# Latent depthwise convolution on 32x64 array tiles, and the scan's decay rows loaded from ScalarE's queue

## The chip, the cores and the metric

The kernel runs on one core of one Trainium2 chip. A core has a matrix engine (TensorE, "PE" in the profile; its loads of the stationary operand are "PEld"), VectorE ("DVE"), ScalarE ("ACT"), GpSimd ("POOL") and a queue processor (SyncE, "SP") that here issues all DMAs. Each engine works through its own list of instructions in order, and semaphores tie the lists together. The metric is the device time of the whole kernel in microseconds (us), as the median of several runs; less is better.

## The reference, cut to what matters

One layer of a diffusion backbone is applied to 256 context tokens and to 2048 latent tokens, which form a grid of 32 rows by 64 columns. An input projection feeds two branches: a bidirectional state-space scan (SSD) and a Conformer branch; an output projection joins them. The change touches two places, the depthwise convolution of the Conformer branch on the latent grid, and a load in the scan.

```
def depthwise_conv(x, w, b):            # w: 31 taps x 1024 channels
    k, ch = w.shape
    out = lax.conv_general_dilated(x, w.reshape(k, 1, 1, ch), window_strides=(1, 1),
        padding=((k // 2, k // 2), (0, 0)), dimension_numbers=('NHWC', 'HWIO', 'NHWC'),
        feature_group_count=ch)
    return out + b

def conformer_branch(ga, gb, conv_w, conv_b, ln_g, ln_b):   # latent: (1, 32, 64, 1024)
    h = ga * jax.nn.sigmoid(gb)
    h = depthwise_conv(h, conv_w, conv_b)
    h = layer_norm(h, ln_g, ln_b)
    return jax.nn.silu(h)
```

The taps run along the grid's rows only. So for one channel the convolution is a product of the 64 x 32 grid (columns by rows) with a banded 32 x 32 matrix that is made of that channel's taps. In the scan, per head and chunk of 128 tokens, `decay_in = exp(segsum(la))` is a 128 x 128 matrix, made from one row of running sums (the decay row) that is laid over all partitions.

## The kernel before, in words

Tokens come in 18 tiles of 128 (two of context, sixteen latent). The work has two halves: tiles 0 to 9, then 10 to 17. In each half a phase of the input projection (`xbc_phase`) feeds the scan, and a second one (`post`: `gab_unit` for the gates, `silu_unit` for the rest) runs while the scan of that half (`scan`, `pass_a`) is woven in between its matmuls. The projection's matmuls are L378 to L380, three for each 128-row slice, with 512 moving columns. They give TensorE a dense stream, and everything else is put between them by hand: `interleave` and `merge` advance the generators of the scan and of the convolutions one step at a time after so many projection steps. The framework then orders each engine's list by a simulated timeline on the basis of that order (`schedule_with_timeline_sim=True`). After the second half come the output projection and the norms (L1078 and what is around it), to the end.

The latent convolution runs in the second half only, 8 groups of 128 channels (`lat_conv`, L603 to L645), one after another, with the context convolution (`ctx_conv`, VectorE) between them; the list of these steps (`extra`) is merged with 63 scan steps over 344 projection steps. A group does this:

- L607 loads the bias rows; L611 loads `kd`, for each channel its 32 x 32 band matrix, read with overlapping rows from the padded taps; L616 loads `cx`, the gated grid, from `GL` in DRAM, where `gab_unit` (L540) stored it. Partition `c4*32 + r` holds grid row `r` of every fourth channel, so the four 32-partition quarters hold four channels. `kd` and `cx` have one buffer each (`bufs=1`).
- `expand` (L622): ScalarE copies the small matrices onto the diagonal of a zeroed 128 x 128 operand (`kbuf`, two buffers, cleared once by GpSimd), so that one matmul serves four channels at once. Four copies make the operand for 8 matmul calls, 16 copies a group.
- L634: 32 calls a group; the stationary operand is the grid (128 x 64), the moving one the block-diagonal matrix (128 x 128), the result 64 grid columns by 4 channels x 32 rows. The halves `h` go to the lower and the upper 64 result partitions. A call in plain float32 appears in the profile as two instructions.
- L639: VectorE evicts each result bank, halves it, adds the bias and writes it in the order row, channel (`cvv`); L644 stores that to `CVL` in DRAM.

The scan's step (`pass_a`): `load_lb` (L664) loads the decay rows of 4 heads, broadcast to 128 partitions, into `lb`, one tile for each direction, each with 4 buffers, 8 loads a token tile. `mask` (ScalarE L673, GpSimd L676), `decay` (ScalarE L684, 4 exponentials) and `mix` (VectorE L688, L689) turn them into decay matrices, and `diag` (TensorE L720) uses them. A buffer is free again after L688 (one direction) or L720 (the other). Result banks are split in 3 ("mm", for the projection) and 5 ("ss", for everything else: `px`, `py`, `po`, `pst`, `pb` of the scan, `cps`, and the convolution's `cp`).

```
    extra = chain(f for j in range(4) for f in (lat_conv(2 * j, lp, kbuf), ctx_conv(j + 4, cg), lat_conv(2 * j + 1, lp, kbuf)))
    interleave(take(blocks, 344), merge(sc_, 63, extra, 8 * 6 + 4 * 13), 344)
```

Of the kernel before, what the change touches and what calls it, by code (L numbers as in the profile page):

```python
# [17 lines left out]
P = 128  # L18
# [49 lines left out]
def backbone_kernel(ctx, tc, xa, xt_in, cols, rows, wconv, conf_b, gp_row, bg_row, state0, w_mod, w_dt, w_in, w_out,  # L68
# [458 lines left out]

    def gab_unit(half, j, hb):
        wb = next_w()
        wa = next_w()  # L530
        for b in ORDER[half]:
            BN, o = BNS[b], TOK[b]
            pg = bank("mm", f"gb{half}_{j}_{b}")
            yield from mm_cm(pg, wb, hb[b])
            th = ev(f"gth{half}_{j}_{b}")[:, :BN]
            S.activation(th, pg[:, :BN], AF.Tanh, scale=0.5)  # L536
            pa_ = bank("mm", f"ga{half}_{j}_{b}")
            yield from mm_cm(pa_, wa, hb[b])
            V.scalar_tensor_tensor(th, th, 1.0, pa_[:, :BN], ADD, MUL)  # L539
            DMA.dma_start(GL[j][:, o:o + BN], th)  # L540

# [61 lines left out]
    def lat_conv(j, lp, kbuf):  # L603
        cbb = lp.tile([P, HD], F32, tag="cbb", name=f"cbb{j}", bufs=2)
        for h in range(2):
            c0 = j * P + h * 64
            DMA.dma_start(cbb[h * 64:(h + 1) * 64], conf_b[c0:c0 + 64].partition_broadcast(64))  # L607
        kd = lp.tile([P, 32, 32], F32, tag="kd", name=f"kd{j}", bufs=1)
        for c4 in range(4):
            src = bass.AP(tensor=wconv.tensor, offset=(j * 4 + c4) * 64 * 32, ap=[[32, 32], [1, 1024]])  # L610
            DMA.dma_start(kd[c4 * 32:(c4 + 1) * 32].rearrange("p r g -> p (r g)"), src)  # L611

        x = lp.tile([P, 32, 64], F32, tag="cx", name=f"cx{j}", bufs=1)
        src = GL[j][:, 256:].rearrange("(g c) (r w) -> c r g w", c=4, w=64)
        for c4 in range(4):
            DMA.dma_start(x[c4 * 32:(c4 + 1) * 32], src[c4])  # L616

        def expand(u):
            kt = kbuf[u % 2]
            for c4 in range(4):  # L620
                rs = slice(c4 * 32, (c4 + 1) * 32)
                S.copy(kt[rs, :, rs].rearrange("p (h q) r -> p h q r", h=2),  # L622
                       kd[rs].rearrange("p r (h u q) -> p u h q r", h=2, u=4)[:, u])

        vt = lp.tile([P, 32, HD], F32, tag="cvv", name=f"cvv{j}", bufs=1)
        yield
        expand(0)
        yield
        for u in range(4):
            kt = kbuf[u % 2]  # L630
            ps = bank("ss", f"cp{j}_{u}")
            for q in range(4):
                for h in range(2):
                    T.matmul(ps[h * 64:(h + 1) * 64, q * P:(q + 1) * P], x[:, h * 16 + u * 4 + q, :], kt[:, h * 4 + q, :],  # L634
                             start=True, stop=True)
            if u < 3:
                expand(u + 1)
            yield
            V.scalar_tensor_tensor(vt[:, ::-1, u * 16:(u + 1) * 16].rearrange("p r c -> p c r"),  # L639
                                   ps.rearrange("p (c r) -> p c r", r=32), 0.5,  # L640
                                   cbb[:, u * 16:(u + 1) * 16].unsqueeze(2).to_broadcast([P, 16, 32]), MUL, ADD)
# [3 lines left out]
        yield  # L645


    def pass_a(i):
# [11 lines left out]
        def load_lb(g, hq):  # L660
            for d in range(2):
                lb = pa.tile([P, 4, P], F32, tag=f"lb{d}", name=f"lb{i}{g}{hq}{d}", bufs=4)
                r0 = il * 32 + d * NH + g * 8 + hq * 4
                DMA.dma_start(lb.rearrange("p h l -> p (h l)"),  # L664
# [197 lines left out]
    def chain(gens):  # L862
        for g in gens:
            yield from g
# [64 lines left out]
    kbuf = [lp.tile([P, 8, P], F32, name=f"kbuf{u}") for u in range(2)]  # L929
    for u in range(2):  # L930
        G.memset(kbuf[u], 0.0)
    blocks = post(1, 5)
    cg = lambda name: lp.tile([P, D], F32, tag="cg", name=name, bufs=2)
    extra = chain(f for j in range(4) for f in (lat_conv(2 * j, lp, kbuf), ctx_conv(j + 4, cg), lat_conv(2 * j + 1, lp, kbuf)))
# [295 lines left out]
```

## Time and profile before

| what | value |
|---|---|
| median of 3 runs | 1877.12 us (1874.78 to 1882.59) |
| the profiled execution: time | 1882.2 us |
| its span, first to last instruction | 1880.5 us |
| its mean granted TensorE clock | 0.986 |
| matmuls of the latent convolution (L634) | 512, from 957.8 to 1336.9 us |
| ScalarE's copies for them (L622) | 128, 83.3 us busy |
| loads of decay rows (L664) | 144, on SP's queue |
| first scan beside the projection | about 275 to 700 us |
| second scan, with the latent convolution | about 935 to 1340 us |

How to read the profile. Rows of groups have the line, engine and operation, the tiles as out<-in, the shape (partitions x elements) and the count; behind the first bar the busy time in us and the mean duration of one in ns, behind the second the engine's idle time just before them and what ended it. For matmuls the shape begins with rows*columns of the stationary operand. Rows of a stretch give for each engine its busy time and, in brackets, its instructions, then the granted TensorE clock, the busy share of the DMA engines and GB/s. Rows in order of time begin with start and duration in us; a count at the end means that so many of a kind were put together, from the first start to the last end. Rows of one tile give the shortest, the median and the longest duration in ns. Rows of waits give who waited for whom: us in total, how often, the longest. "SPq" is SP's list, where the duration is what it took to issue a DMA.

### The profile page before, as it was taken

To read this page: it belongs to the slowest core of one execution; us is meant where nothing else is said; L and a number is where in the kernel's file an instruction comes from. 1 tells how busy PE (TensorE), PEld (TensorE's weight loads), DVE (VectorE), ACT (ScalarE), POOL (GpSimd) and SP (SyncE) were. 2 spreads that over 40 slices of the span, in tenths; PEclk is the share of its full clock that TensorE was granted. 3 is DMA by queue.
4 is the path that set the end of the run, shared out by engine and by line. 5 is a ranking of instruction groups with operands and counts; after the bars stand their busy time and mean duration, and the time that the engine had idled before them with its cause. 6 is when DMAs were issued, how large, how long until landed. Compare 5 with 4: busy or idle time off the path is not lost.

```text
span 1880.5 us, 26833 instructions
## 1 busy us (share of the span) xinstructions
PE 1825.6 (97%) x9739; PEld 1504.6 (80%) x9739; DVE 1188.2 (63%) x1699; ACT 839.5 (45%) x1786; POOL 269.0 (14%) x351
## 2 busy tenths in 40 slices
PE   7899999999999999999999899999999999999998
PEld 4788887787887888888877677777887888888887
DVE  2477887776545553577585768655427676766662
ACT  3646424443455441644355666675414232232321
POOL 0002001111111100100001011110013333333220
PEclk9899999999999999999999999999999999999999
DMA  8556575564677754545587897978887655555532
GB/s 302 212 200 198 211 239 179 176 222 155 211 269 225 225 200 169 165 154 188 179 195 215 210 242 194 278 185 234 239 268 239 191 174 173 165 172 173 175 102 78
DMA packets 290400, 375.29 MB, mean 200 GB/s; under 512 B 85206, under 2 KB 187478, under 8 KB 290268
## 3 DMA queue, kind: packets, MB, share of 16 engines
q1 hardware_dynamic: 290268, 373.58, 64.2%
q8 instruction: 77, 1.26, 0.3%
q14 instruction: 55, 0.45, 0.1%
HBM read 243.92 MB, written 129.59 MB: 199 GB/s over the span
## 4 chain that ended last, share of the span: by engine, by line
PE 62%; DMA 5%; ACT 3%; issue 3%; DVE 2%; SPq 2%; POOL 0%; POOLq 0%; DVEq 0%; ACTq 0%
PE op L1078 20%; PE sp L378 6%; PE sp L379 6%; PE sp L380 6%; DMA lb<-lt 3%; PE xp L379 2%; PE xp L378 2%; PE xp L380 2%; PE py L720 2%; PE ga L378 2%; PE ga L380 1%; PE po L727 1%; PE ga L379 1%; PE qo L985 1%; PE gb L378 1%
## 5 line engine op out<-in xcount | busy, mean ns | idle before, releaser
L684 ACT ACTIVATE lb<-lb,WB 128x128 f32<-128x128 f32 x576 | 184.1, 391 | 150.9 <-POOL lb L676 149.0
L378 PE MATMUL sp<-hh,wh 128*128 128x512 f32 (+1 forms) x640 | 239.7, 375 | 2.6 <-DVE sth L550 2.6
L379 PE MATMUL sp<-hl,wh 128*128 128x512 f32 (+1 forms) x640 | 237.0, 370 | 0.0
L380 PE MATMUL sp<-hh,wl 128*128 128x512 f32 (+1 forms) x640 | 236.7, 370 | 0.2 <-DMA wl<-wld 0.2
L676 POOL TENSOR_SCALAR_AFFINE_SELECT lb<-lb 128x512 f32<-128x512 f32 x144 | 108.7, 760 | 749.7 <-ACT el L673 416.1
L378 PE MATMUL xp<-hh,wh 128*128 128x512 f32 (+1 forms) x480 | 179.1, 375 | 6.1 <-ACT wh L353 4.0
L379 PE MATMUL xp<-hl,wh 128*128 128x512 f32 (+1 forms) x480 | 179.1, 373 | 0.2 <-DVE hl L299 0.2
L380 PE MATMUL xp<-hh,wl 128*128 128x512 f32 (+1 forms) x480 | 179.2, 374 | 0.0
L475 DVE SCALAR_TENSOR_TENSOR cva<-raw,cwh,cva 128x1280 f32<-128x1280 f32 (+1 forms) x96 | 142.7, 1495 | 15.5 <-ACT cva L469 13.6
L378 PEld LDWEIGHTS sp<-hh,wh 128*128 128x128 f32 x640 | 121.0, 189 | 24.3 <-DVE sth L550 3.1
L380 PEld LDWEIGHTS sp<-hh,wl 128*128 128x128 f32 x640 | 121.0, 189 | 21.6 <-DMA wl<-wld 0.7
L379 PEld LDWEIGHTS sp<-hl,wh 128*128 128x128 f32 x640 | 121.2, 189 | 20.1 <-issue 0.5
L378 PE MATMUL gb<-hh,wh 128*128 128x512 f32 (+1 forms) x320 | 121.9, 381 | 3.4 <-DVE gth L539 3.4
L378 PE MATMUL ga<-hh,wh 128*128 128x512 f32 (+1 forms) x320 | 120.4, 376 | 2.6 <-ACT gth L536 2.6
L379 PE MATMUL gb<-hl,wh 128*128 128x512 f32 (+1 forms) x320 | 119.3, 373 | 0.0
L380 PE MATMUL gb<-hh,wl 128*128 128x512 f32 (+1 forms) x320 | 119.1, 372 | 0.0
L380 PE MATMUL ga<-hh,wl 128*128 128x512 f32 (+1 forms) x320 | 118.1, 369 | 0.0
L379 PE MATMUL ga<-hl,wh 128*128 128x512 f32 (+1 forms) x320 | 117.9, 369 | 0.0
L590 DVE SCALAR_TENSOR_TENSOR cg<-cg,cv 128x256 f32<-128x256 f32 x240 | 113.3, 497 | 2.5
L550 DVE SCALAR_TENSOR_TENSOR sth<-sth,sp 128x512 f32<-128x512 f32 (+1 forms) x80 | 50.4, 630 | 98.4 <-ACT sth L549 98.4
L378 PEld LDWEIGHTS xp<-hh,wh 128*128 128x128 f32 x480 | 92.0, 192 | 23.0 <-ACT wh L353 4.8
L688 DVE TENSOR_TENSOR lb<-lb,lb 128x512 f32<-128x512 f32 x72 | 51.6, 717 | 85.6 <-ACT lb L684 55.8
(219 smaller groups left out, 3860.8 us busy)
## 6 DMA issues: line engine op xcount, KB each, us to landing
lb<-lt SPq DMA_DIRECT2D x144, 256.0 KB, 4.2
wr<-in_w_in SPq DMA_DIRECT2D x88, 256.0 KB, 4.9
whd<-wh SPq DMA_DIRECT2D x44, 512.0 KB, 3.4
wld<-wl SPq DMA_DIRECT2D x44, 512.0 KB, 4.7
wh<-whd SPq DMA_DIRECT2D x44, 512.0 KB, 5.2
wl<-wld SPq DMA_DIRECT2D x44, 512.0 KB, 5.6
xT<-xb SPq DMA_DIRECT2D x18, 512.0 KB, 5.4
yp<-yg SPq DMA_DIRECT2D x36, 256.0 KB, 4.5
```

The source lines that it names most:

```text
L378: T.matmul(ps[:, :BN], wh[:, k, :], hh[:, k, :], start=(k == 0), stop=False)
L379: T.matmul(ps[:, :BN], wh[:, k, :], hl[:, k, :], start=False, stop=False)
L380: T.matmul(ps[:, :BN], wl[:, k, :], hh[:, k, :], start=False, stop=(k == KT - 1))
L475: V.scalar_tensor_tensor(a[:, :n], raw[:, t:t + n], cwh[:, ct * 5 + t:ct * 5 + t + 1], a[:, :n], MUL, ADD)
L550: V.scalar_tensor_tensor(th, th, 1.0, ps[:, :BN], ADD, MUL)
L590: V.scalar_tensor_tensor(acc, g[:, t:t + 256], cv[:, w0 + t:w0 + t + 1], acc, MUL, ADD)
L676: G.affine_select(E[g, hq, d], E[g, hq, d], pattern=[[0, 4], [sg, P]], compare_op=ALU.is_ge, fill=NEG, base=0, channel_multiplier=-sg)
L684: S.activation(lb[:, h, :], lb[:, h, :], AF.Exp, bias=WB[:, i, c + h:c + h + 1])
L688: V.tensor_tensor(a, a, E[g, hq, 1], ADD)
L720: T.matmul(py[g][j * HD:(j + 1) * HD, q * P:(q + 1) * P], xt[g][:, h * HD:(h + 1) * HD], E[g, hq, 0][:, t, :], start=True, stop=True)
L727: T.matmul(po[g][:, q * P:(q + 1) * P], Sf[g][:, q * P:(q + 1) * P], bc[:, 2 + g, :], start=True, stop=True)
L1078: T.matmul(pso[n], lhs[:, k % 8, :], w[:, n * 512:(n + 1) * 512], start=(k == 0 and m == 0), stop=(k == 15 and m == 2))
```

## The change

The convolution no longer expands its matrices. Each of the four 32-partition quarters (one channel each) is now a matmul of its own, 32 contraction rows by 64 result partitions, with 32 moving columns: 128 calls a group in place of 32. Quarters `a` and `a + 1` go to two "ss" banks that are taken together; the order is by channel `q`, half `h`, quarter `a`. One ScalarE copy a group (`kt`) turns the band matrices into channel-major, row-reversed order; before, the reversal was made by VectorE's write in L639. The loads are a function of their own (`lat_load`), `kd` and `cx` have two buffers, and group `j + 1` is loaded during group `j` if its gates have been written (`gl_done`). A group has 6 steps in place of 7, so that `extra` has 96 steps in place of 104. In the scan, `load_lb` issues its DMAs on ScalarE's queue.

```diff
--- before.py
+++ after.py
@@ -525,9 +525,12 @@
         for _ in dtp:
             pass
 
+    gl_done = set()
+
     def gab_unit(half, j, hb):
         wb = next_w()
         wa = next_w()
+        gl_done.discard(j)
         for b in ORDER[half]:
             BN, o = BNS[b], TOK[b]
             pg = bank("mm", f"gb{half}_{j}_{b}")
@@ -538,6 +541,8 @@
             yield from mm_cm(pa_, wa, hb[b])
             V.scalar_tensor_tensor(th, th, 1.0, pa_[:, :BN], ADD, MUL)
             DMA.dma_start(GL[j][:, o:o + BN], th)
+        if half:
+            gl_done.add(j)
 
     def silu_unit(half, c0, dst, j, hb, order=None):
         w = next_w()
@@ -600,49 +605,53 @@
         yield
 
 
-    def lat_conv(j, lp, kbuf):
+
+
+    lat_in = {}
+
+    def lat_load(j, lp):
+        kd = lp.tile([P, 32, 32], F32, tag="kd", name=f"kd{j}", bufs=2)
+        x = lp.tile([P, 32, 64], F32, tag="cx", name=f"cx{j}", bufs=2)
         cbb = lp.tile([P, HD], F32, tag="cbb", name=f"cbb{j}", bufs=2)
+        lat_in[j] = kd, x, cbb
         for h in range(2):
             c0 = j * P + h * 64
             DMA.dma_start(cbb[h * 64:(h + 1) * 64], conf_b[c0:c0 + 64].partition_broadcast(64))
-        kd = lp.tile([P, 32, 32], F32, tag="kd", name=f"kd{j}", bufs=1)
-        for c4 in range(4):
-            src = bass.AP(tensor=wconv.tensor, offset=(j * 4 + c4) * 64 * 32, ap=[[32, 32], [1, 1024]])
-            DMA.dma_start(kd[c4 * 32:(c4 + 1) * 32].rearrange("p r g -> p (r g)"), src)
-
-        x = lp.tile([P, 32, 64], F32, tag="cx", name=f"cx{j}", bufs=1)
-        src = GL[j][:, 256:].rearrange("(g c) (r w) -> c r g w", c=4, w=64)
-        for c4 in range(4):
-            DMA.dma_start(x[c4 * 32:(c4 + 1) * 32], src[c4])
-
-        def expand(u):
-            kt = kbuf[u % 2]
-            for c4 in range(4):
-                rs = slice(c4 * 32, (c4 + 1) * 32)
-                S.copy(kt[rs, :, rs].rearrange("p (h q) r -> p h q r", h=2),
-                       kd[rs].rearrange("p r (h u q) -> p u h q r", h=2, u=4)[:, u])
-
+        src = GL[j][:, 256:].rearrange("(g a) (r w) -> a r g w", a=4, w=64)
+        for a in range(4):
+            rs = slice(a * 32, (a + 1) * 32)
+            DMA.dma_start(kd[rs].rearrange("p r g -> p (r g)"),
+                          bass.AP(tensor=wconv.tensor, offset=(j * 4 + a) * 64 * 32, ap=[[32, 32], [1, 1024]]))
+            DMA.dma_start(x[rs], src[a])
+
+    def lat_conv(j, lp, more):
+        if j not in lat_in:
+            lat_load(j, lp)
+        kd, x, cbb = lat_in.pop(j)
+        yield
+        kt = lp.tile([P, 32, 32], F32, tag="kt", name=f"kt{j}", bufs=1)
+        S.copy(kt[:, :, ::-1].rearrange("p g r -> p r g"), kd)
+        if more(j + 1):
+            lat_load(j + 1, lp)
+        yield
         vt = lp.tile([P, 32, HD], F32, tag="cvv", name=f"cvv{j}", bufs=1)
-        yield
-        expand(0)
-        yield
-        for u in range(4):
-            kt = kbuf[u % 2]
-            ps = bank("ss", f"cp{j}_{u}")
-            for q in range(4):
+        for a2 in (0, 2):
+            ps = {a: bank("ss", f"cp{j}_{a}") for a in (a2, a2 + 1)}
+            for q in range(16):
                 for h in range(2):
-                    T.matmul(ps[h * 64:(h + 1) * 64, q * P:(q + 1) * P], x[:, h * 16 + u * 4 + q, :], kt[:, h * 4 + q, :],
-                             start=True, stop=True)
-            if u < 3:
-                expand(u + 1)
+                    for a in ps:
+                        rs = slice(a * 32, (a + 1) * 32)
+                        T.matmul(ps[a][h * 64:(h + 1) * 64, q * 32:(q + 1) * 32], x[rs, h * 16 + q, :], kt[rs, h * 16 + q, :],
+                                 start=True, stop=True)
             yield
-            V.scalar_tensor_tensor(vt[:, ::-1, u * 16:(u + 1) * 16].rearrange("p r c -> p c r"),
-                                   ps.rearrange("p (c r) -> p c r", r=32), 0.5,
-                                   cbb[:, u * 16:(u + 1) * 16].unsqueeze(2).to_broadcast([P, 16, 32]), MUL, ADD)
+            for a in ps:
+                V.scalar_tensor_tensor(vt[:, :, a::4].rearrange("p r c -> p c r"),
+                                       ps[a].rearrange("p (c r) -> p c r", r=32), 0.5,
+                                       cbb[:, a::4].unsqueeze(2).to_broadcast([P, 16, 32]), MUL, ADD)
+            yield
         for h in range(2):
             c0 = j * P + h * 64
             DMA.dma_start(CVL[:, c0:c0 + 64].rearrange("(r w) c -> w r c", w=64), vt[h * 64:(h + 1) * 64])
-        yield
 
 
     def pass_a(i):
@@ -661,7 +670,7 @@
             for d in range(2):
                 lb = pa.tile([P, 4, P], F32, tag=f"lb{d}", name=f"lb{i}{g}{hq}{d}", bufs=4)
                 r0 = il * 32 + d * NH + g * 8 + hq * 4
-                DMA.dma_start(lb.rearrange("p h l -> p (h l)"),
+                S.dma_start(lb.rearrange("p h l -> p (h l)"),
                               LT[half][r0:r0 + 4, :].rearrange("h l -> (h l)").partition_broadcast(P))
                 E[g, hq, d] = lb
 
@@ -926,12 +935,10 @@
     ph_b[0].close()
     ph_l = ExitStack()
     lp = ph_l.enter_context(tc.tile_pool(name="lp", bufs=1, side="right"))
-    kbuf = [lp.tile([P, 8, P], F32, name=f"kbuf{u}") for u in range(2)]
-    for u in range(2):
-        G.memset(kbuf[u], 0.0)
     blocks = post(1, 5)
     cg = lambda name: lp.tile([P, D], F32, tag="cg", name=name, bufs=2)
-    extra = chain(f for j in range(4) for f in (lat_conv(2 * j, lp, kbuf), ctx_conv(j + 4, cg), lat_conv(2 * j + 1, lp, kbuf)))
+    lat = lambda j: lat_conv(j, lp, gl_done.__contains__)
+    extra = chain(f for j in range(4) for f in (lat(2 * j), ctx_conv(j + 4, cg), lat(2 * j + 1)))
     sc_ = scan(range(9, NT))
     run(take(blocks, 24))
     interleave(take(blocks, 24), [sc_] * 4, 24)
```

## The prediction

> **What bounds the kernel now.** I read the page's totals first, then busy time by stretch, then the stretch that holds the change: who waits for whom, the chain of waits, the order of time of SP and TensorE.
>
> ```profile
> span 1880.5 us, 26833 instructions
> PE 1825.6 (97%) x9739; PEld 1504.6 (80%) x9739; DVE 1188.2 (63%) x1699; ACT 839.5 (45%) x1786; POOL 269.0 (14%) x351
> ```
>
> TensorE is busy for 97% of the span, no other engine for more than 63%. So the time moves by what changes on TensorE: its own work, its idle time, and the clock that it loses by idling. Two stretches of equal length follow, the first scan and the second; only the second holds the latent convolution. Then three pieces of the second.
>
> ```profile
> core 0: us, PE busy (x) PEld busy (x) DVE busy (x) ACT busy (x) POOL busy (x), PEclk, DMA share, GB/s
> 310.00:693.00 383.00, 374.32 (x2120) 313.53 (x2119) 236.34 (x426) 181.63 (x460) 43.28 (x62) 0.99 0.62 203
> 957.00:1340.00 383.00, 365.55 (x2207) 285.93 (x2206) 253.75 (x413) 241.44 (x546) 42.55 (x64) 0.98 0.81 219
> 1000.00:1050.00 50.00, 45.27 (x261) 34.97 (x259) 33.28 (x56) 29.65 (x76) 7.51 (x13) 0.93 0.63 198
> 1150.00:1200.00 50.00, 45.28 (x273) 36.20 (x272) 33.15 (x55) 32.20 (x73) 4.57 (x7) 0.93 1.01 238
> 1250.00:1300.00 50.00, 46.46 (x273) 36.01 (x273) 31.32 (x47) 35.15 (x73) 3.81 (x6) 0.97 1.04 239
> ```
>
> The second scan leaves TensorE idle for 383 - 365.55 = 17.5 us, and in three pieces it also runs at a granted clock of 0.93, 0.93 and 0.97: 50 x (0.07 + 0.07 + 0.03) = 8.5 us more. These 26 us are the most that removing waits here can give. The next rows, by line, say whose they are: the convolution's matmuls (L634), and the copies that build their operand on ScalarE (L622).
>
> ```profile
> L634 PE MATMUL cp<-kbuf,cx 128*64 128x128 f32 x512 | 37.1, 291 | 12.4 <-ACT kbuf L622 10.0 <-DMA cx<-gl 1.9 <-DVE cvv L639 0.3
> L622 ACT COPY kbuf<-kd 32x256 f32<-32x256 f32 x128 | 83.3, 657 | 19.6 <-DMA kd<-in_wconv 11.8 <-PE cp L634 6.0
> ```
>
> Of the 17.5 us idle, 12.4 stand in front of these matmuls, 10.0 of them waiting for the copies. Why the copies are late shows in SP's queue, then in the chain and in TensorE's order of time:
>
> ```profile
> 1050.52 5.19 SPq L644 DMA_DIRECT2D cvl<-cvv  x2
> 1055.77 3.84 SPq L616 DMA_DIRECT2D cx<-gl  x2
> 1059.70 1.93 SPq L664 DMA_DIRECT2D lb<-lt  x1
> ```
>
> ```profile
> 1062.92 3.89 DMA lb<-lt
> 1066.84 0.42 ACT el L673
> 1067.70 1.28 ACT lb L684 x4
> 1070.64 0.52 ACT kbuf L622
> ```
>
> ```profile
> 1037.36 0.39 PE L379 MATMUL gb<-hl,wh 128*128 128x512 f32 x1
> 1037.58 0.39 PE L380 MATMUL gb<-hh,wl 128*128 128x512 f32 x1
> 1040.64 1.68 PE L634 MATMUL cp<-kbuf,cx 128*64 128x128 f32 x14 [2.67 <-ACT kbuf L622]
> ```
>
> One after another: the store of one convolution (5.19 us to issue two), the loads of the next (3.84), then a decay row block; ScalarE waits for it in its exponentials, and the copies stand behind these. TensorE, which otherwise starts a matmul each 0.22 us, stands for 2.67 us.
>
> **The change part by part.** *The matmuls themselves.* Before, 8 channel groups x 32 calls give 512 instructions (two to a call). Now it is 8 x 128 calls, so 2048 instructions, of 32 moving columns in place of 128, with 64 stationary columns as before, in four array tiles in turn (two row quarters by two column halves). No row shows a row tile, so I bound the price by its nearest rows.
>
> ```profile
> L634 PE MATMUL cp<-kbuf,cx x512: 272/273/476, 957.8 to 1336.9; 128*64 128x128 f32 x171
> 1068.49 0.40 PE L735 MATMUL pst<-xwh,btl 128*128 128x512 f32 x1
> 1068.82 1.09 PE L634 MATMUL cp<-kbuf,cx 128*64 128x128 f32 x16
> 1069.84 0.49 PE L380 MATMUL ga<-hh,wl 128*128 128x512 f32 x1
> L239 PE MATMUL mp<-wm,sc x128: 378/379/634, 13.6 to 34.9; 128*2 128x256 f32 x128
> 28.03 0.61 PE L239 MATMUL mp<-wm,sc 128*2 128x256 f32 x8
> L727 PEld LDWEIGHTS po<-bc,Sf x272: 186/192/338, 327.4 to 1317.1; 128*128 128x128 f32 x136
> 1067.03 0.97 PEld L727 LDWEIGHTS po<-bc,Sf 128*128 128x128 f32 x8 [0.17 <-issue]
> L248 PEld LDWEIGHTS mc<-ident,mr x16: 133/136/206, 25.6 to 51.8; 2*128 2x128 f32 x16
> 27.69 0.32 PEld L248 LDWEIGHTS mc<-ident,mr 2*128 2x128 f32 x4 [0.44 <-issue]
> ```
>
> The old ones: 16 in 1.09 us, the last taking 0.273, so (1.09 - 0.273) / 15 = 54.5 ns apart: 512 x 54.5 = 27.9 us. Two column halves run at a time, so each holds its half for 109 ns, and a quarter of the columns would hold it 27. Loads of 128 stationary columns: (0.97 - 0.192) / 7 = 111 ns apart, so 56 for 64 columns (estimate). Then a tile is held by its load: 56 ns. Four tiles do work at once where they are column tiles: 8 instructions of 256 columns end within 0.61 us, (0.61 - 0.379) / 7 = 33 ns apart, although one takes 379. With four tiles in step: 56 / 4 = 14 ns, 2048 x 14 = 28.7 us, **+1 us**; I take this, as the load row and the four-tile row are the nearest. Lower end: loads into few rows are quicker, (0.32 - 0.136) / 3 = 61 ns for 128 columns, 31 for 64, hence 7.7 ns and 16 us: -12. Upper ends: only the column halves overlap, 28 ns, 57 us: +29; nothing overlaps, 56 ns, 115 us: +87 (rivals).
>
> The Trainium skill speaks against this edit: its page "TensorEngine Tiling (Array Packing)", section "Instruction Overhead", gives a matmul about 60 cycles of overhead and advises against taking the tiling factor out of a dimension that is already small. 32 columns lie under that; at 2.4 GHz it is 25 ns (estimate), and 2048 would cost 51 us, so that the sum would come out 22 us higher. No row here shows so small a matmul in a long run.
>
> *Changes of array mode.* Entering and leaving shows in the rows just quoted: 0.33 us from L735 to the first of the 16, and 1069.84 - (1068.82 + 1.09 - 0.27) = 0.20 us from the last start to L380, against 0.22 and 0.055 in sequence: some 0.25 us for a burst. There were 32 bursts, now there are 16 of 128; but a neighbour on 128x64 tiles (the scan's L720) now also changes mode. 16 x 0.25 = 4, of which I take **-3 us**.
>
> *ScalarE's copies.* 128 copies (83.3 us) become 8 of 128x1024. Price:
>
> ```profile
> L1019 ACT CAST yh<-y 128x1024 fp32r<-128x1024 f32 x18 | 19.0, 1053 | 24.8 <-DVE y L1013 23.9
> L784 ACT COPY cb<-pb 128x256 f32<-128x256 f32 x18 | 6.7, 373 | 12.4 <-DVE btl L783 12.2
> ```
>
> Plain, 1.05 us each; the old ones read with a stride and took 657 against 373 ns, so up to 1.9 with the new strided writes: 8 to 15 us. About 70 us leave ScalarE in the second scan, where it is busy for 241 of 383. One copy stands before 128 calls, in a step of its own; before, four stood before each 8. The memset of the two expansion buffers goes too, off the path.
>
> *Loads ahead.* The kernel tile and the grid tile get two buffers and are asked for during the convolution before, if their gate rows have all been written; counting steps (96 over 344), that holds for six of the eight. One SP wait goes with it:
>
> ```profile
> SPq L611 <- ACT kbuf L622: 24.1, 7, 7.5
> SPq L664 <- DVE lb L688: 117.5, 43, 8.6
> SPq L664 <- PE py L720: 17.9, 15, 2.2
> ```
>
> The 24.1 us in which SP stood for the kernel tile's only buffer are gone, and what queued behind (decay rows, weights, stores) comes earlier. So of the 12.4 us in front of L634 I take off **-11**, and of the 8.5 us of clock, which follow the long waits, **-6**; of the other 5 us of idle time **-2**. Vector's 32 evictions keep their number and shape: 0.
>
> *Decay rows on ScalarE's queue.* 144 issues, half of them in each scan:
>
> ```profile
> L664 SPq DMA_DIRECT2D lb<-lt x144: 319/360/2937, 152.2 to 1291.4; - x144
> DMA to landing us min/median/max: 3.2/4.2/8.7
> ```
>
> 72 x 0.36 = 26 us of ScalarE in each scan: in the second less than the copies free, in the first hidden in 383 - 182 us of idle time. They leave the queue of the convolution's long stores and loads. But each still waits for its buffer (117.5 + 17.9 us in all, on SP), and now the evictions and exponentials on ScalarE stand behind. Three "mm" banks cover TensorE for some microseconds; without that cover the whole would be 135 us. Two result banks are also taken at once from the five "ss" banks. For both I put **+4 us** in the second scan; for the first 0, with ends -6 (its late rows come earlier) and +12.
>
> Sum: +1 - 3 - 11 - 6 - 2 + 4 = -17 us. The profiled execution took 1882.2 us (span 1880.5 and 1.7 around it), so it would take 1865; it lies 5.1 above the median of the runs, 1877.1, and from this the forecast is 1860.
>
> **The rivals.** *Loads of the four tiles follow one another (slower).* The price is the spacing on TensorE: at 56 ns 115 us in place of 28, 1860 + 86 = 1946. It decides from 22 ns on: (27.9 + 18) / 2048, where the gain of 18 without this term is used up. For: no row has two row tiles at once. Against: column tiles overlap fully in the rows above, and the old pairs kept 54.5 ns with loads of 56. Chance 0.07.
>
> *A floor between matmul starts, or halves only.* The closest average in the rows is 33 ns (the four column tiles): 68 us, 1899. With only halves overlapping, 28 ns, 57 us: 1888. Against: 33 ns there is set by 256 columns. Chance 0.15 for 24 to 33 ns: 1881 to 1899. The skill's rule above belongs here; its 25 ns would give 1882.
>
> *ScalarE held up in SP's place.* 58 waits, on average 2.3 us, with exponentials and evictions behind them. For: ScalarE is in the scan's chain. Against: SP ran ahead and had to wait, where ScalarE comes later. If a ninth reached TensorE, +15: 1875. Chance 0.12.
>
> *The waits only move:* the two banks taken at once, or stores and loads that still fill SP's queue, give the 17 us back; 1877. For: the DMA share is 1.01 and 1.04 in two pieces, and the bytes stay. Chance 0.08.
>
> **How the numbers follow.** The forecast case has 0.58; its own range is 1840 (the 16 us of matmuls and most of the 26 us gone) to 1872. What a measurement can tell from no change is about 0.5%, 9.4 us. Faster, under 1868: nearly all of the forecast case and the edges of two rivals, 0.61. Slower, over 1886: the serial case and over half of the floor, 0.17. Same: 0.22. The range 1840 to 1892 leaves out the serial case, the floor's upper part and a little below.
>
> **What would show it.** Right: the new matmuls about 14 ns apart and near 29 us in all, idle time before them under 2 us, a granted clock of 0.99 in the second scan, ScalarE busy there for 190 to 200 us, 16 bursts. Wrong: matmul starts over 22 ns apart; ScalarE waiting long in its DMA issues with TensorE idle behind tanh evictions; the first scan longer.

## The result, and the profile after

The changed kernel takes 1948.18 us (median of 4 runs, 1942.29 to 1949.42) against 1879.86 us of the kernel before on the same chip (4 runs, 1874.78 to 1883.8): ratio 1.0359, 95% interval 1.0323 to 1.0395. It is 68 us slower, where 17 us faster was forecast. The profiled execution took 1942.3 us. One of the four executions of no_ahead below fell into a slower state of the chip (2073.7 us, at a granted clock of 0.84 in place of 0.97), and its row leaves that one out.

The totals of the page, then the same two stretches as before (instructions in brackets, then the granted clock), and the stretch from 900 us to the end of the projection (1419.9 us before, 1481.6 after), first of the kernel before and then of the changed one:

```profile
span 1940.5 us, 29728 instructions
PE 1838.2 (95%) x11275; PEld 1519.8 (78%) x11275; DVE 1191.4 (61%) x1699; ACT 774.5 (40%) x1666; POOL 257.3 (13%) x349
```

```profile
310.00:693.00 383.00, 375.00 (x2126) 314.84 (x2125) 241.90 (x435) 182.35 (x459) 43.65 (x61) 0.99 0.62 205
957.00:1340.00 383.00, 319.40 (x3154) 252.75 (x3147) 220.92 (x367) 156.00 (x390) 40.69 (x61) 0.91 0.72 184
```

```profile
900.00:1419.90 519.90, 502.21 (x2830) 0.98 0.81 221
```

```profile
900.00:1481.60 581.60, 516.37 (x4359) 0.94 0.72 198
```

TensorE's work in the first scan is unchanged (375.00 us busy, 374.32 before). All of the loss lies in the second: its projection ends 61.7 us later. TensorE stands idle for 581.60 - 516.37 = 65.2 us there in place of 17.7, that is 47.5 us more. The other 14.2 us are busy time; the granted clock is 0.94 in place of 0.98, so the same matmuls take longer: between 957 and 1430 us those of `ga` on L378 average 439 ns in place of 404.

Next the matmuls themselves: in order of time, and by tile with the evictions.

```profile
1034.82 0.41 PE L644 MATMUL cp<-kt,cx 32*64 32x32 f32 x6
1035.65 2.05 PE L644 MATMUL cp<-kt,cx 32*64 32x32 f32 x122 [0.42 <-DVE yg L770]
```

```profile
L644 PE MATMUL cp<-kt,cx x2048: 217/218/312, 956.3 to 1378.3; 32*64 32x32 f32 x187
L648 DVE SCALAR_TENSOR_TENSOR cvv<-cp,cbb x32: 1003/1048/1114, 964.5 to 1379.5; 128x512 f32<-128x512 f32 x32
```

And the evictions of the kernel before:

```profile
L639 DVE SCALAR_TENSOR_TENSOR cvv<-cp,cbb x32: 1014/1067/1107, 960.2 to 1340.8; 128x512 f32<-128x512 f32 x32
```

122 matmuls in 2.05 us, the last of them 0.218 long: 1.83 / 121 = 15.1 ns apart, where 14 was forecast. The price is right, so the loss isn't here. But the first eviction starts at 964.5, 8.2 us after the first matmul; before, it was 960.2 - 957.8 = 2.4 us. That shows in what TensorE waits for (groups between 957 and 1430 us, behind the second bar the idle time):

```profile
L378 PE MATMUL ga<-hh,wh 128*128 128x512 f32 x103 | 45.2, 439 | 11.8 <-DMA wh<-whd 10.6 <-ACT gth L539 1.2
L644 PE MATMUL cp<-kt,cx 32*64 32x32 f32 x2012 | 38.2, 229 | 14.9 <-DVE cvv L648 9.3 <-issue 4.1 <-ACT sb L758 1.1
L742 PE MATMUL pst<-xwh,bth 128*128 128x512 f32 x36 | 18.2, 504 | 13.0 <-DVE cvv L648 6.3 <-ACT sb L758 4.4 <-DVE yo L750 1.4
L705 PE MATMUL px<-ident,xT 128*128 128x128 f32 x64 | 10.6, 293 | 16.7 <-DVE cvv L648 16.5 <-PE pb L782 0.3
```

The name `cvv` stands in three of the four rows: 9.3 + 6.3 + 16.5 = 32.1 us in which a next matmul waits for the bank that an eviction of the convolution has yet to empty. Two such waits in order of time (VectorE, then TensorE), and a third with its cause:

```profile
1059.55 3.09 DVE L595 SCALAR_TENSOR_TENSOR cg<-cg,cv 128x256 f32<-128x256 f32 x6
1062.55 1.87 DVE L648 SCALAR_TENSOR_TENSOR cvv<-cp,cbb 128x512 f32<-128x512 f32 x2
...
1082.96 0.69 DVE L697 TENSOR_TENSOR lb<-lb,lb 128x512 f32<-128x512 f32 x1 [7.26 <-ACT lb L693]
1083.57 1.89 DVE L648 SCALAR_TENSOR_TENSOR cvv<-cp,cbb 128x512 f32<-128x512 f32 x2
```

```profile
1063.66 0.39 PE L644 MATMUL cp<-kt,cx 32*64 32x32 f32 x2 [4.10 <-issue]
1064.48 3.63 PE L644 MATMUL cp<-kt,cx 32*64 32x32 f32 x126 [0.43 <-DVE cvv L648]
...
1077.11 0.30 PE L644 MATMUL cp<-kt,cx 32*64 32x32 f32 x2
1084.63 3.63 PE L644 MATMUL cp<-kt,cx 32*64 32x32 f32 x126 [7.23 <-DVE cvv L648]
```

```profile
1213.19 0.84 ACT L682 ACTIVATE el<-lb 64x256 f32<-64x256 f32 x2 [2.27 <-DMA lb<-lt]
1214.10 1.23 POOL L685 TENSOR_SCALAR_AFFINE_SELECT lb<-lb 128x512 f32<-128x512 f32 x2 [4.48 <-DMA lb<-lt]
1214.77 2.45 ACT L693 ACTIVATE lb<-lb,WB 128x128 f32<-128x128 f32 x8 [0.73 <-POOL lb L685]
1217.30 0.69 DVE L697 TENSOR_TENSOR lb<-lb,lb 128x512 f32<-128x512 f32 x1 [7.58 <-ACT lb L693]
1217.91 1.89 DVE L648 SCALAR_TENSOR_TENSOR cvv<-cp,cbb 128x512 f32<-128x512 f32 x2
1218.97 0.71 PEld L705 LDWEIGHTS px<-ident,xT 128*128 128x128 f32 x4 [8.29 <-DVE cvv L648]
```

The burst that began at 1063.66 is done by 1068.1; its evictions start at 1083.57. On VectorE's list they stand behind taps of the context convolution (L595) and behind a `mix` of the scan (L697), which waits for the decay chain. In the meantime the next burst has issued 2 of its 128 matmuls and stands for its second bank, and with it everything behind it on TensorE's list; at 1218.97 it is a `px` that stands.

One measure is used below: the time for which a bank of the convolution is held, from the first matmul of its burst to the end of its eviction, over all 32 evictions, and in it the lag from the burst's last matmul to the start of the eviction. Before: held 6.0 us on average (191 us in all), lag 3.7. After: held 14.1 (452 in all), lag 10.0. From the last matmul of a pair to the first of its two evictions, the 16 waits add up to 153 us. VectorE is busy for 95 of them, with 93 taps and 29 instructions of `mix` among other things. In most of the rest it stands still: 23 us in front of `mix`, which waits for ScalarE's exponentials, and 16 us in front of `xwl` (L720), which waits for another result of ScalarE. So an eviction whose bank is full stands behind instructions that are not yet ready to run.

### The profile page after: what moved, and what is told of

Its sections match the earlier page's. It is cut to its first block, busy times and chain, and to the rows that moved or that the text cites. A ratio compares the mean times of both kernels' runs of the same rounds, so it can differ in the third digit from the quotient of the medians.

```text
span 1940.5 us, 29728 instructions
## 1 busy us (share of the span) xinstructions
PE 1838.2 (95%) x11275; PEld 1519.8 (78%) x11275; DVE 1191.4 (61%) x1699; ACT 774.5 (40%) x1666; POOL 257.3 (13%) x349
## 5 line engine op out<-in xcount | busy, mean ns | idle before, releaser
L378 PE MATMUL sp<-hh,wh 128*128 128x512 f32 (+1 forms) x640 | 239.4, 374 | 4.1 <-DVE sth L555 4.1
L378 PE MATMUL xp<-hh,wh 128*128 128x512 f32 (+1 forms) x480 | 179.0, 374 | 6.4 <-ACT wh L353 5.1
L378 PEld LDWEIGHTS sp<-hh,wh 128*128 128x128 f32 x640 | 121.0, 189 | 24.9 <-DVE sth L555 4.9
L378 PE MATMUL ga<-hh,wh 128*128 128x512 f32 (+1 forms) x320 | 125.0, 391 | 15.0 <-DMA wh<-whd 10.6
L378 PE MATMUL gb<-hh,wh 128*128 128x512 f32 (+1 forms) x320 | 122.6, 383 | 5.6 <-DVE gth L542 4.7
L595 DVE SCALAR_TENSOR_TENSOR cg<-cg,cv 128x256 f32<-128x256 f32 x240 | 111.2, 488 | 3.4
L378 PEld LDWEIGHTS xp<-hh,wh 128*128 128x128 f32 x480 | 92.0, 192 | 23.1 <-ACT wh L353 5.7
L697 DVE TENSOR_TENSOR lb<-lb,lb 128x512 f32<-128x512 f32 x72 | 51.3, 713 | 92.6 <-ACT lb L693 75.7
```

Source lines behind the costliest of these rows:

```text
L378: T.matmul(ps[:, :BN], wh[:, k, :], hh[:, k, :], start=(k == 0), stop=False)
L595: V.scalar_tensor_tensor(acc, g[:, t:t + 256], cv[:, w0 + t:w0 + t + 1], acc, MUL, ADD)
L697: V.tensor_tensor(a, a, E[g, hq, 1], ADD)
```

## The experiments

In the table, ratios to the kernel before, run on the same chip, with the 95% interval; "held" and "lag" as above, and "idle" TensorE's idle time from 900 us to the projection's end, all in us from each kernel's profile. The kernel before has 6.0, 3.7 and 18 in these columns.

| kernel | median, us | ratio | held | lag | idle |
|---|---|---|---|---|---|
| changed | 1948.2 | 1.0359 (1.0323 to 1.0395) | 14.1 | 10.0 | 65 |
| conv_only | 1949.3 | 1.0365 (1.0338 to 1.0391) | 13.8 | 9.2 | 69 |
| rows_only | 1880.2 | 0.9996 (0.9983 to 1.0009) | 5.6 | 3.4 | 19 |
| rows_pool | 1938.2 | 1.0311 (1.0283 to 1.0339) | 11.5 | 7.8 | 54 |
| one_bank | 1920.6 | 1.0221 (1.0198 to 1.0244) | 9.7 | 6.4 | 23 |
| before_pairs | 1883.4 | 1.0021 (1.0002 to 1.0040) | 7.7 | 3.9 | 26 |
| no_ahead | 1944.8 | 1.0358 (1.0326 to 1.0390) | 13.9 | 10.0 | 62 |
| act_evict | 1948.3 | 1.0367 (1.0344 to 1.0390) | 13.8 | 10.0 | 67 |
| kept_order | 1884.6 | 1.0019 (1.0005 to 1.0033) | 6.1 | 2.9 | 27 |
| split_pairs | 1946.5 | 1.0343 (1.0321 to 1.0366) | 10.9 | 3.4 | 31 |
| kept_before | 1877.7 | 0.9986 (0.9967 to 1.0005) | 3.6 | 1.4 | 22 |
| few_calls | 1867.6 | 0.9925 (0.9899 to 0.9952) | 8.8 | 6.2 | 25 |
| kept_sp | 1891.2 | 1.0049 (1.0031 to 1.0066) | 5.8 | 2.4 | 27 |
| kept_pool | 1883.5 | 1.0012 (0.9998 to 1.0026) | 4.4 | 1.2 | 21 |
| kept_pool_stores | 1899.1 | 1.0101 (1.0076 to 1.0125) | 4.9 | 1.7 | 24 |
| kept_conv_act | 1912.9 | 1.0173 (1.0146 to 1.0199) | 5.9 | 2.1 | 42 |

**Which of the two parts.** Theory A: the decay rows on ScalarE's list. Theory B: the convolution, through the banks that it holds.

conv_only is the changed kernel with SP's queue for the decay rows, rows_only the kernel before with ScalarE's, rows_pool the changed kernel with GpSimd's:

```diff
-                S.dma_start(lb.rearrange("p h l -> p (h l)"),
+                DMA.dma_start(lb.rearrange("p h l -> p (h l)"),
```

> The changed kernel with the decay rows back on SP's queue; the convolution stays as changed. Theory A (the decay rows on ScalarE's list: there the 4.2 us of landing stand between a load and its use, and whatever ScalarE waits for delays the load): all of the 68 us is gone, and the convolution alone gives what was forecast without the 4 us put down for that edit, 1856 to 1866 us. Theory B (the convolution: two result banks taken at once, held until VectorE's two evictions, so that the scan's px, pst and po wait for a bank): little changes, 1930 to 1950 us, with px still idle some 16 us behind L648. Theory C (they need each other): between 1885 and 1925.

> The kernel before with the decay rows on ScalarE's queue and nothing else. Theory A: slower by 60 us or more, 1940 to 1970 us, since the 83 us of expansion copies also stand in ScalarE's list; ScalarE idle for long behind the landing of lb in the second scan. Theory B: the time of before, 1872 to 1888 us. Theory C: 1885 to 1925.

> The changed kernel with the decay rows on GpSimd's queue, which is busy for 13% and whose L685 is the first user of them together with ScalarE. Theory A in its narrow form (ScalarE's list is the place that hurts, because evictions and exponentials stand behind the load): 1860 to 1880 us. Theory A in its wide form (any engine that takes part in the scan's chain and reaches the load late puts the landing into the chain): 1920 to 1950 us. Theory B: 1930 to 1950 us.

The row part alone does nothing that can be measured (0.9996), the convolution alone makes the whole loss (1.0365). Theory A falls, and so does the C of these three runs (the parts need each other). With GpSimd's queue the median is 10 us below the changed kernel's, but the two intervals overlap.

**Banks in pairs, loads ahead, the evicting engine.** one_bank takes the quarters singly, before_pairs makes the kernel before take pairs, no_ahead drops the prefetch, act_evict lets ScalarE evict:

```diff
-        for a2 in (0, 2):
-            ps = {a: bank("ss", f"cp{j}_{a}") for a in (a2, a2 + 1)}
+        for a1 in range(4):
+            ps = {a1: bank("ss", f"cp{j}_{a1}")}
```

```diff
-        if more(j + 1):
-            lat_load(j + 1, lp)
```

```diff
-                V.scalar_tensor_tensor(vt[:, :, a::4].rearrange("p r c -> p c r"),
...
+                S.mul(vt[:, :, a::4].rearrange("p r c -> p c r"), ps[a].rearrange("p (c r) -> p c r", r=32), 0.5)
...
+        V.tensor_tensor(vt, vt, cbb.unsqueeze(1).to_broadcast([P, 32, HD]), ADD)
```

> The changed kernel, but a quarter takes its bank alone: four steps of 64 matmul instructions and one eviction, in place of two steps of 128 and two evictions; steps, loads and everything else as changed. A bank was held on average 14.1 us there (first matmul to the end of its eviction, 32 banks, 452 us in all) against 6.0 us before (191 us in all). Theory B (the loss is the time for which the convolution holds banks that TensorE's next work needs, because two are taken at once and both wait for VectorE): the banks are held under 8 us, the waits of px, pst and cp for cvv are gone, and the time is 1870 to 1905 us, of which up to 29 us are the matmuls with only two tiles at work (14 to 28 ns apart). Theory C (the loads ahead, which changed SP's queue): 1935 to 1960. Theory D (2048 small matmuls cost time beside what they are busy, whatever the banks): 1940 to 1975.

> The kernel before, with its expansion and its 512 matmuls, but two groups of 16 channels take their banks together: two bursts of 32 instructions in place of four of 16, and both evictions after the next step, as in the changed kernel. Theory B: banks are held 12 us or more and the time goes to 1915 to 1950 us. Theories C and D: 1875 to 1890, as before.

> The changed kernel without the loads ahead: each group loads its grid and matrices at its own start, as before; both still have two buffers. Theory B: no change from the changed kernel but the waits for its own loads, 1940 to 1960 us. Theory C: the loss is gone, 1860 to 1890. Theory D: 1940 to 1960.

> The changed kernel, pairs of banks as there, but ScalarE evicts them (halved), and VectorE adds the bias afterwards for a whole group of 128x2048 in SBUF. VectorE's other work (92 taps of the context convolution at 0.48 us and 34 of the scan's mixes stood in the 16 gaps between the last matmul of a pair and its eviction) no longer delays a bank. Theory B: banks are held 4 to 9 us in place of 14 and the time is 1865 to 1905 us, unless ScalarE's own list makes the evictions wait as long. Theories C and D: 1935 to 1960.

Theory C (loads ahead) falls with no_ahead. Theory B is hit only in part: its range for one_bank ended at 1905 us, and 7.0 us of `px`'s waits for `cvv` are left there. With single banks TensorE's idle time is back at 23 us, though the banks are still held 9.7 us; with two tiles at a time the matmuls alone keep TensorE busy for 69 us, 32 more than before, and that fits most of what is lost at 1921. Its row in order of time shows why, where 122 took as long in pairs:

```profile
960.25 2.05 PE L644 MATMUL cp<-kt,cx 32*64 32x32 f32 x64
```

(2.05 - 0.218) / 63 = 29 ns apart, twice the 15 of four tiles. But pairs on the kernel before cost 4 us, not 40: there the lag stays at 3.9. And ScalarE evicts no sooner than VectorE did (lag 10.0): on its list 101 exponentials of the decay matrices stand in the 16 gaps. So neither the pair nor the engine makes the loss alone. What is common to changed, conv_only, no_ahead and act_evict is a lag of 9 to 10 us, and the next theory is about that.

**The place in the list.** Theory E: the framework puts the evictions too far back in VectorE's list. kept_order adds one ordering rule on VectorE's list and no other edit; what the program states after an eviction is issued behind it. The framework then lays out all lists anew, so other instructions change places too (219 of ScalarE's 1666 stand in another order than in the changed kernel):

```diff
+            behind.close()
             for a in ps:
-                V.scalar_tensor_tensor(vt[:, :, a::4].rearrange("p r c -> p c r"),
+                ev = V.scalar_tensor_tensor(vt[:, :, a::4].rearrange("p r c -> p c r"),
...
+            behind.enter_context(tc.issue_after(ev.ins))
```

kept_before has the same in the kernel before; split_pairs is before_pairs with four calls of 32 columns in place of each of 128:

```diff
+                        for c in range(0, P, 32):
+                            T.matmul(ps[u][h * 64:(h + 1) * 64, q * P + c:q * P + c + 32], x[:, h * 16 + u * 4 + q, :],
+                                     kt[:, h * 4 + q, c:c + 32], start=True, stop=True)
```

> The changed kernel with one thing more: on VectorE's list, what the program states after an eviction of the convolution may not be put ahead of it (an order alone, no wait for it). Pairs of banks, bursts of 128 instructions, loads and steps are as changed. Measured so far: the lag from the last matmul of a burst to its eviction is 3.7 us with bursts of 16 instructions (before), 6.4 with 64 (one bank alone), 10.0 with 128 (changed), and VectorE is busy for most of it with taps and mixes that the framework put ahead. Theory E (it is the place in VectorE's list: the framework's own timeline makes a burst of many instructions long, and so puts its eviction too late): lag under 5 us, TensorE's idle time from 900 us to the projection's end falls from 65 to under 30 us, time 1862 to 1890. Theory B as it stood (two banks at once are too many, wherever the eviction stands): 1930 to 1955.

> The kernel before with pairs of banks (1883 us) and each of its matmul calls of 128 moving columns made as four calls of 32: 2048 instructions, bursts of 128, all on 128-row tiles, with the expansion as before; the result is the same. The matmuls themselves cost up to 29 us more (two column halves, 28 ns apart, estimate from loads of 56). Theory E: the lag goes from 3.9 to 8 us or more, TensorE's idle time from 26 to over 45 us, time 1930 to 1965. Theory F (the loss comes with the row quarters or with what went with them: 32-row tiles, one ScalarE copy, no expansions between the bursts): the lag stays near 4 and the time is 1905 to 1920.

> The kernel before with its evictions kept in order on VectorE's list in the same way. Its lag is 3.7 us already. Theory E: little to gain, 1868 to 1882 us; if it comes out under the changed kernel with kept order, the new convolution brings nothing even in its best place. Theory B says nothing on it: 1875 to 1885.

kept_order brings 64 of the 68 us back, with pairs, bursts of 128, 2048 matmuls and the loads ahead all left as changed. Its list in order of time, and its groups between 957 and 1430 us (the evictions are L650 here):

```profile
1163.20 2.07 PE L645 MATMUL cp<-kt,cx 32*64 32x32 f32 x128
1165.31 1.98 DVE L650 SCALAR_TENSOR_TENSOR cvv<-cp,cbb 128x512 f32<-128x512 f32 x2 [2.96 <-PE cp L645]
1167.15 0.38 DVE L593 TENSOR_SCALAR cg<-cg,cv,cfb 128x256 f32<-128x256 f32 x1
1167.45 0.68 DVE L700 TENSOR_TENSOR lb<-lb,lb 128x512 f32<-128x512 f32 x1
```

```profile
L645 PE MATMUL cp<-kt,cx 32*64 32x32 f32 x2048 | 33.1, 218 | 0.0
L745 PE MATMUL pst<-xwh,bth 128*128 128x512 f32 x36 | 18.0, 501 | 9.4 <-ACT sb L761 7.7 <-ACT kt L634 1.7
L708 PE MATMUL px<-ident,xT 128*128 128x128 f32 x64 | 10.1, 282 | 12.4 <-issue 7.2 <-DVE cvv L650 2.6 <-PE pb L785 1.1
```

VectorE now waits 2.96 us for the burst, empties the banks 0.04 us after it, and takes the tap and the mix afterwards. In front of the convolution TensorE doesn't wait at all (14.9 us as changed, 12.4 before), and in these rows 2.6 us are left of the 32 for `cvv`. Theory E holds for the loss, and theory D (small matmuls cost time whatever the banks) falls, since all 2048 are still there. Against kept_before (0.9986), which has the same ordering rule, the new convolution in its best place is no gain.

split_pairs misses what theory E said of it: its lag is 3.4, not 8. It fills its two banks one after the other, so that the first eviction can come before the burst ends; counted from the last matmul of each bank itself, the lag is 5.3 (before_pairs 4.7). Its time is nearly as long for another reason: on 128-row tiles its matmuls alone keep TensorE busy for 87 us, 50 more than before, where up to 29 were expected. From the first matmul to the eviction, though, it takes 9.8 us; the burst itself, 6.4 us on average, fills most of that. Counted so, the times rise with the instructions of a burst where the framework's own order stands: 4.9 us with 16 (before), 6.7 with 32 (before_pairs), 8.6 with 64 (one_bank), 9.8 and 13.1 with 128 (split_pairs, changed). The same 128 instructions give two different times, so theory F, that what came with the row quarters also counts, isn't ruled out.

**Why so far back.** few_calls has a quarter of the instructions, for as many columns:

```diff
-            for q in range(16):
+            for q in range(4):
...
-                        T.matmul(ps[a][h * 64:(h + 1) * 64, q * 32:(q + 1) * 32], x[rs, h * 16 + q, :], kt[rs, h * 16 + q, :],
-                                 start=True, stop=True)
+                        g = h * 16 + q * 4
+                        T.matmul(ps[a][h * 64:(h + 1) * 64, q * P:(q + 1) * P], x[rs, g, :],
+                                 kt[rs, g:g + 4, :].rearrange("p g r -> p (g r)"), start=True, stop=True)
```

> The changed kernel (framework's own order) with a quarter of its matmul calls, each with 128 moving columns in place of 32: bursts of 32 instructions for two banks in place of 128, as many columns in all. It leaves out the right grid for three channels of four (each call takes the grid of its first channel for four), so only its time counts. Theory E1 (the framework's timeline prices a burst by its instructions, and that puts the eviction late): from the first matmul to the eviction 8 us or less in place of 13.1, TensorE's idle time under 40 us, time 1870 to 1905. Theory E2 (priced by its columns, or the place has another reason): 12 to 14 us, idle 55 to 70, time 1925 to 1945.

7.7 us from the first matmul to the eviction and 25 us idle are as E1 says; 1867.6 us lies 2.4 below its range. The number of instructions in a burst moves the place in the list (the lag goes from 10.0 to 6.2), and that fits a timeline that makes a small matmul longer than the 15 ns which it takes. No run here shows the framework's own prices, so this last link is argued and not shown. That the time is below the kernel before fits its fewer calls: its matmuls keep TensorE busy for 20 us, kept_order's for 33, those of the kernel before for 37.

**What is left.** kept_order takes the wait for the operand away and prices the matmuls as forecast, and still stands at 1.0019. Three theories: H, the decay rows on ScalarE's list; J, SP's queue, with the convolution's transfers ahead of the scan's; K, waits that only change places. kept_sp and kept_pool move the decay rows' loads as conv_only and rows_pool did. kept_pool_stores also puts the scan's stores (`yp`, `st`) on GpSimd's queue, and kept_conv_act puts the convolution's loads and stores on ScalarE's; in both the decay rows are on GpSimd's.

> Kept order, with the decay rows' loads back on SP's queue. In kept order ScalarE stood 10.7, 9.8, 9.3, 7.1 and 5.5 us (42 us) while its next load of a decay row waited for another DMA to land (a store or load of the convolution that uses the same semaphore), and TensorE stood 7.7 us for ScalarE's eviction of pst. Theory H (with the evictions in their place, the decay rows on ScalarE's list now cost what the trace shows there): those waits leave ScalarE, time 1864 to 1878 us. Rival I (the loads then wait as long on SP, behind 4 to 5 us of the convolution's loads and stores, and the scan is as late): 1879 to 1890, no change from kept order.

> Kept order, with the decay rows' loads on GpSimd's queue, whose list holds little but the masks that follow these loads. Theory H: 1862 to 1878 us, as with SP's queue or a little better, since the loads stand behind neither ScalarE's work nor the convolution's transfers. Rival I: 1879 to 1890.

> Kept order with the decay rows' loads on GpSimd's queue, and the scan's two stores (yp, st) there too, so that no load or store of the scan's inner steps but xT and bc stands on SP behind the convolution's transfers. With the loads alone on GpSimd, VectorE stood 12.8 us for one store of yp that SP issued after 5.09 us of the convolution's loads, and px stood 9.2 us of TensorE's time in that stretch. Theory J (what keeps kept order at 1884 is SP's queue, in which the convolution's transfers stand ahead of the scan's): 1862 to 1876 us. Theory K (TensorE's idle time of some 20 to 27 us only changes its place among the scan's waits, and the new convolution has nothing left to give): 1877 to 1890.

> Kept order with the decay rows' loads on GpSimd's queue, and the convolution's own loads and stores on ScalarE's queue. ScalarE has the room (174 us busy of 383), but it takes 4 to 5 us for four loads of the grid on SP, and its exponentials stand behind. Theory J: 1862 to 1880 us, if ScalarE's list does not become the scan's wait. Theory K: 1877 to 1890. If ScalarE's issues hold up the exponentials: over 1890.

H falls: with SP's queue the median is 7 us above that with ScalarE's (the intervals just touch, and 1891.2 lies 1 us above rival I's range too), and GpSimd's makes no difference to ScalarE's that the intervals can tell. J falls: the stores on GpSimd and the convolution's transfers on ScalarE both make it slower. kept_conv_act came out as its last case said: ScalarE spends 107 us on issuing DMAs between 957 and 1340 us (27 in kept_order), and TensorE waits 8.9 us for its `gth` alone. In kept_pool_stores `px` is down to 6.4 us, but a weight load from SP's queue is late:

```profile
L378 PE MATMUL ga<-hh,wh 128*128 128x512 f32 x112 | 46.2, 412 | 14.0 <-DMA wh<-whd 14.0
```

So the waits do change places, as K says, but K is not shown: its range of 1877 to 1890 us missed both kernels for which it was stated. Each edit also makes the framework lay out the lists anew, which these runs don't separate from the queues. What keeps kept_order from a gain stays open. No version that does the whole computation ran faster than the kernel before by more than a measurement can tell; kept_before, with 0.9986, comes nearest.

## Why the prediction was wrong

- *The step that failed* is "Vector's 32 evictions keep their number and shape: 0". Number and shape did stay (32 of 1.05 us). Their place in VectorE's list didn't: from 3.7 us behind the burst to 10.0. The next matmuls that needed a bank stood for it, 32.1 us in the three rows above, and the granted clock fell with them. The one ordering rule of kept_order, which puts the evictions back in their place, is worth 64 us. The term next to it, "two result banks are also taken at once", had the right object: pairs alone cost 4 us in before_pairs, and the rest came with the late evictions. The rival of the two banks was given 17 us and a chance of 0.08.
- *The matmuls, +1 us:* right. The spacing is 15.1 ns against 14 (31 us for 2048, where 28.7 was expected), and where nothing makes them wait 33.1 us busy against 37.1 before. Four row and column tiles do work at once, with 15.1 ns between starts; two take 29 ns. The rivals of serial loads and of a floor at 24 to 33 ns fall. So does, as a price between any two matmuls, the rule of the Trainium skill's page "TensorEngine Tiling (Array Packing)", section "Instruction Overhead": its 60 cycles (25 ns at 2.4 GHz, estimate) are not seen between starts on four tiles; for one tile, which starts every 58 to 60 ns, these runs don't contradict it. The same page of the Trainium skill says in its section "Gotcha 1: PSUM Pressure" that row tiles put more pressure on PSUM and write to different banks. The changed kernel does take two banks at once and holds them for 452 us against 191, but kept_order, with the same row tiles, holds them for 194: the tiles alone didn't cost that.
- *The wait for the operand, -11:* the wait did go, as the 0.0 us of kept_order show. Whether the loads ahead were needed for it is not shown: no_ahead, which still has the second buffers and the one copy, doesn't wait for its operand either (11.6 us there, 7.2 of them for `cvv` and 4.1 without a cause in the profile). In the changed kernel 14.9 us stand in the same place for another reason.
- *The clock, -6, and other idle time, -2:* wrong in sign, since both follow the waits. The clock is 0.91 where 0.99 was expected.
- *ScalarE:* a copy takes 2.08 us where up to 1.9 was expected, and 839.5 - 774.5 = 65 us leave it over the whole span (70 expected). The 190 to 200 us expected in the second stretch seem to count 26 us of issuing, which the profile doesn't count as busy; without them they are 171, and kept_order has 175. The 156 us of the changed kernel are lower because its work ends 62 us later and so less of it falls into that stretch.
- *The decay rows, 0 in the first scan:* right (375.00 against 374.32), and 0.9996 for the part alone. ScalarE wasn't the wait that was feared.
- *That the gain of 17 us comes once the waits in front of L634 go:* wrong even with the evictions in their place. In kept_order 12.4 us in front of the convolution went, and `px` and `pst` wait 12.4 and 9.4 us, where the same groups of the kernel before have 2.7 and 0.3:

```profile
L733 PE MATMUL pst<-xwh,bth 128*128 128x512 f32 x36 | 17.8, 495 | 0.3 <-DVE yo L741 0.3
L696 PE MATMUL px<-ident,xT 128*128 128x128 f32 x64 | 10.1, 283 | 2.7 <-issue 2.0 <-PE pb L773 0.6
```

With the evictions in place, the result is that of the rival "the waits only move" (1877 us, chance 0.08), though neither of the two grounds given for it is shown. A reading that fits, and is not shown either, is that the idle time read as the price of one wait belonged to a chain with other waits close behind.

## What to carry to other kernels

When an edit changes how many instructions stand between two engines, price the place of the consumer in its engine's list as well as its duration, and ask what stands ahead of it that isn't ready yet; the wait shows up at a third instruction, the next one that needs the bank. Look for one name behind the waits of several different instructions: here `cvv` stood behind `px`, `pst` and `cp`. If a framework orders the lists, test that order by itself (one ordering constraint) before giving up an edit whose own instructions cost what they should.

## What the runs showed of the hardware

- Row tiles are as independent as column tiles: matmuls of 32x64 stationary values and 32 columns started 15.1 ns apart with four tiles in turn and 29 ns with two, so about 60 and 58 ns apart on a tile.
- An engine that issues DMAs can stand for another queue's transfer. In kept_order ScalarE's list shows this (the second row holds two issues of decay rows, from the first to the end of the second):

```profile
1135.58 2.04 ACT L634 COPY kt<-kd 128x1024 f32<-128x1024 f32 x1
1137.26 10.98 ACTq L676 DMA_DIRECT2D lb<-lt  x2
1148.34 0.62 ACT L722 CAST xwh<-xw 128x512 fp32r<-128x512 f32 x1 [10.72 <-DMA cvl<-cvv]
```

Between the two issues it stood for the landing of a store of the convolution, a transfer that SP had issued, with which its load has only the semaphore in common (number 103 in the trace: the store landed on it at 1147.81, and the second load was issued at 1147.88). Taking these loads off ScalarE didn't make the kernel faster, so this cost is not one that decides here.
